# Second block's recurrence: preparations and scans at a higher scheduler's priority

## The chip, the core and the metric

The kernel runs on one core of a Trainium2 chip. Its engines are TensorE (PE in the profile, with its weight loads as PEld), VectorE (DVE), ScalarE (ACT), GpSimd (POOL) and SyncE (SP, which issues most DMAs). The metric is the device time of one execution in microseconds; an execution that was profiled has its own time beside the span of its trace.

## The reference, cut to what matters

The model is a first block (two layers of mixers with feed-forwards, not touched here) and a second block. The second block projects 512 tokens of width 1024 by w_in (RWKV columns and columns of a short convolution), runs a bidirectional recurrence of 8 heads of 64 over them, projects out and goes through 16 experts. The change concerns the recurrence:

```python
px = modulate_2(rmsnorm(x, norm1_g[l]), sh1, sc1) @ w_in[l]
xr, xk, xv, xw, xa, xgl = split_rwkv(px_rw, shift_mu[l], grid_shift(px_rw, rows))
# rwkv_bidir, for each direction d (forward, reversed), from the context's states:
decay = jnp.exp(-jnp.exp(heads(wl)))
a = heads(jax.nn.sigmoid(a0[d] + xa @ a_up[d]))
kd = k * (1 + (a - 1) * k_a_h)
def step(s, inp):
    r_t, w_t, k_t, v_t, a_t, b_t = inp
    sa = jnp.einsum('bhvk,bhk->bhv', s, a_t)
    s = s * w_t[:, :, None, :] + sa[..., :, None] * b_t[:, :, None, :] + v_t[..., :, None] * k_t[:, :, None, :]
    return s, jnp.einsum('bhvk,bhk->bhv', s, r_t)
# then group norm, bonus, gate, and
x = x + g1 * (jnp.concatenate([a_x, b_x], axis=-1) @ w_out[l])
x = x + g2 * expert_choice_ffn(hx, router_w[l], ...)
```

## The kernel before

The kernel computes the recurrence in chunks of 64 tokens, for two groups of four heads, both directions side by side on the partitions. For a group, `rwkv_prep` makes the operands of all eight chunks, and `rwkv_scan` runs over the chunks one after another.

`rwkv_prep` goes from the shifted k, r, v to transposes of v (L1819), sums of squares (L1840), two small projections (L1863, L1869), and then, for each head, a chain on VectorE and ScalarE that begins at L1866 and has a prefix scan (L1876). PE makes the bonus (L1903) and the products of chunk by chunk (L1930, L1981, L1991, flips L1786, L2005). Last comes the inverse of a unit triangular matrix for each chunk and head: VectorE transposes its blocks (L2045), works through 62 small operations and transposes again (L2062, L2081, L2082); ScalarE copies four blocks of 32x1024; PE multiplies 32x32 blocks (L2089, L2099). I call this last part the inverse.

`rwkv_scan` does for each chunk on PE L2128, then an addition on VectorE, L2139, a copy on ScalarE, L2148, and an addition that makes the next state, which the next chunk's L2128 needs. Beside this chain stand the chunk's outputs y (PE L2160 and L2161, two additions on VectorE).

The w_in projection is a matmul of f32 by f32 in three terms of a high and a low part: a block of 128 output columns is 24 matmuls of 128x512 (L434, L436, L439). VectorE makes the low part of a weight (`wsplit`, 128x1024), and the shift of a result takes VectorE operations of 128x512 (`shift_blk`). When the first preparation begins, w_in blocks for the second group (k1, r1, v1), for the gate and for the short convolution are left; they are the generators `second` and `convs`.

`weave` runs generators alternately, at rates, so that their instructions are emitted in a braid: preparation 0 with `second`; scan 0 with `convs` and the first eight steps of preparation 1; preparation 1 with `tail`; scan 1 with the rest of `tail`. `tail` is the out projection of the convolution part (`out_f32`, L2302), the normalisation and gate of heads 0 to 3 (`heads_out`, L2245, L1178, L1191, L2259), the out projection of those, and the same for heads 4 to 7 (L2324 onwards) with the routing (`route_setup`, L2365). Between scan 0 and preparation 1 the activations `a` are freed, and `A.move` opens new pools in their place.

What is emitted isn't yet the order of an engine. The framework's scheduler sorts each engine's instructions, by what is ready by its own estimates and by a priority, which is the place in the emitted order unless something raises it. Each engine then executes in the order it was given, one after another. Arithmetic and allocation in these generators are not touched.

Of the kernel before, what the change touches and what calls it, by code (L numbers as in the profile page):

```python
# [16 lines left out]
TL, TC, TA = 512, 256, 768  # L17
# [149 lines left out]
def _run(g):  # L167

    try:
        while True:  # L170
            next(g)
    except StopIteration as e:
        return e.value
# [186 lines left out]
class _K:  # L360
# [1906 lines left out]
    def braid(self, *gs, first=False):  # L2267
# [17 lines left out]
            yield  # L2285
        return out

    def weave(self, *gs, first=False):

        out = _run(self.braid(*gs, first=first))  # L2290
        self.in_zone(0)
        return out
# [138 lines left out]
    def block2(self):  # L2431
# [15 lines left out]
        heads = lambda g: list(range(4 * g, 4 * g + 4))  # L2447
# [10 lines left out]
        def second(k, r, v, bx):  # L2458
            yield from gemms(1, k, r, v)
            xg = self.shift_blk(aa, 13, TL)  # L2460
            self.act(xg.a, xg.a, AF.Tanh, scale=0.5)
            nc.vector.tensor_scalar(xg.a, xg.a, 1.0, None, op0=OP.add)
            yield
            yield from convs(bx, 0, 2)
            return xg

        def convs(bx, n0, n1):
            for n in range(n0, n1):
                bx.append((yield from self.conv2(aa, n)))

        def some(g, n):
            for _ in range(n):
                next(g)
                yield

        B.zone = [0] * 3 + [1] * (8 - 3)
        wa = self.shift_blk(aa, 12, TL, bank=banks.pop(0))
        self.act(wa.a[0:64], wa.a[0:64], AF.Tanh)
        y, bon = [A.new([4, TL], top=True)], [[A.new([TL], top=True) for _ in range(2)]]
        k, r, v = [], [], []  # L2480
# [1 line left out]
        A.reserve(1, 22528)  # L2482
        none = [None, None]
        k1, r1, v1, bon1, bx = list(none), list(none), list(none), list(none), []
        ops0, xg = self.weave((1, 1, self.rwkv_prep(TL, heads(0), r, k, v, wa, bon[0], lambda: y[0].a), 71),
                              (0, 0, second(k1, r1, v1, bx), 15))
        self.free(v)
        A.unreserve(1)
        A.reserve(2, 2048)
        prep = self.rwkv_prep(TL, heads(1), r1, k1, v1, wa, bon1, lambda: y[1].a)  # L2490
        self.weave((2, 1, self.rwkv_scan(TL, 4, ops0, self.S.a[:, 0:4], y[0].a), 12), (0, 0, convs(bx, 2, 4), 5),
                   (0, 0, some(prep, 8), 8))
        self.free(a)
        A.move(53184, 49984, 52672)
# [13 lines left out]
        def tail():  # L2508
            if 0 == 0:
                yield from self.out_f32(I["w2out"], [(4, b)], x, self.P2, 2, True)  # L2510
            o = yield from self.heads_out(0, y[0], bon[0], xg, center, gup)
            yield from self.out_f32(I["w2out"], [(0, o)] if 0 == 0 else [(4, b), (0, o)], x, self.P2, 2, False)
            self.route_setup()

            w = self.load(I["w2out"][:, :, 2:4, :].rearrange("n q k m -> q n k m"), True)
            for cs, nc in ((slice(1, 3), 6), (slice(0, 4, 3), 8)):
                while self.chunks < nc:
                    yield
                o = yield from self.heads_part(1, y[1], bon[1], xg, center, gup, cs)
                yield from self.out_part(w, o, x, self.P2, 2, cs)  # L2520
                yield from self.route(x, cs)
            w.free()
            self.softmax()

        tail = tail()
        ops1 = self.weave((0, 0, prep, 53), (0, 1, tail, 12), first=True)[0]
        self.free([v1[2:], wa])
        self.weave((2, 0, self.rwkv_scan(TL, 4, ops1, self.S.a[:, 4:8], y[1].a), 18), (0, 1, tail, 14))
        self.free([self.S, self.wlora, self.trim, self.rst64])
        A.unreserve(2)  # L2530
        B.zone = [0] * 8
# [253 lines left out]
```

## Time and profile before

| | us |
|---|---|
| median of 3 runs | 3016.4 |
| lowest and highest | 3009.22, 3019.16 |
| profiled execution | 3014.73 |
| its span in the trace | 3013.0 |
| preparation 0 and its inverse | 2065 to 2228 |
| scan 0 | 2228 to 2274 |
| last w_in matmul ends | 2291 |
| preparation 1 and its inverse | 2291 to 2424 |
| scan 1 | 2424 to 2460 |
| rest of the block, routing | 2460 to 2520 |
| experts, to the end | 2520 to 3013 |

The profiled execution's time is 1.7 us above its span and 1.7 us below the median. The stages are read from the trace by the lines named above; they overlap in the program, so each limit is that of the instruction that the stage's chain begins or ends with.

### The profile page before, as it was taken

To read this page: it belongs to the slowest core of one execution; us is meant where nothing else is said; L and a number is where in the kernel's file an instruction comes from. 1 tells how busy PE (TensorE), PEld (TensorE's weight loads), DVE (VectorE), ACT (ScalarE), POOL (GpSimd) and SP (SyncE) were. 2 spreads that over 40 slices of the span, in tenths; PEclk is the share of its full clock that TensorE was granted. 3 is DMA by queue.
4 is the path that set the end of the run, shared out by engine and by line. 5 is a ranking of instruction groups with operands and counts; after the bars stand their busy time and mean duration, and the time that the engine had idled before them with its cause. 6 is when DMAs were issued, how large, how long until landed. Compare 5 with 4: busy or idle time off the path is not lost.

```text
span 3013.0 us, 43714 instructions
## 1 busy us (share of the span) xinstructions
PE 2833.2 (94%) x17880; PEld 2055.9 (68%) x17880; DVE 1667.0 (55%) x2692; ACT 1025.6 (34%) x1657; POOL 257.9 (9%) x237
## 2 busy tenths in 40 slices
PE   7989999999999999999999999979898898999997
PEld 4877557887888878666588777867675664344443
DVE  5856547776576354677664784367846643221113
ACT  5522335511211135544553522256443522001011
POOL 1034320000000010121000000010010111000000
PEclk9999999999999999999999999989999898999998
DMA  6334452366466103111322222203213045999998
GB/s 221 105 105 115 134 187 86 119 208 207 148 223 214 43 31 109 35 37 42 119 71 84 77 91 70 85 31 128 75 47 111 33 155 207 409 409 409 409 409 293
DMA packets 170441, 458.99 MB, mean 152 GB/s; under 512 B 20176, under 2 KB 52560, under 8 KB 169856
## 3 DMA queue, kind: packets, MB, share of 16 engines
q1 hardware_dynamic: 170240, 456.19, 43.1%
q8 instruction: 140, 2.29, 0.3%
q14 instruction: 61, 0.50, 0.1%
HBM read 441.35 MB, written 14.78 MB: 151 GB/s over the span
## 4 chain that ended last, share of the span: by engine, by line
PE 67%; DVE 12%; DMA 5%; ACT 4%; issue 3%; POOL 0%; SPq 0%; DVEq 0%; ACTq 0%; POOLq 0%
PE ps L434 13%; PE ps L436 12%; PE ps L439 12%; PE ps L2642 9%; DVE mem L389 7%; ACT mem L381 4%; PE ps L2625 2%; DVE mem L392 2%; DMA mem<-in_wadt_dram 1%; PE ps L1624 1%; PE ps L610 1%; PE ps L1119 1%; PE ps L1786 1%; PE ps L2302 1%; DMA mem<-in_eu_dram 1%
## 5 line engine op out<-in xcount | busy, mean ns | idle before, releaser
L381 ACT ACTIVATE mem<-mem 128x1024 fp32r<-128x1024 f32 (+16 forms) x837 | 577.4, 720 | 875.5 <-PE ps L439 215.8
L389 DVE TENSOR_TENSOR mem<-mem,mem 128x1024 fp32r<-128x1024 f32 (+17 forms) x596 | 504.0, 862 | 363.9 <-ACT mem L381 166.6
L381 ACT ACTIVATE mem<-ps 128x512 f32<-128x512 f32 (+8 forms) x591 | 302.0, 527 | 930.8 <-PE ps L439 323.3
L434 PE MATMUL ps<-mem,mem 128*128 128x512 f32 (+3 forms) x1991 | 599.0, 358 | 18.0 <-ACT mem L381 13.9
L436 PE MATMUL ps<-mem,mem 128*128 128x512 f32 (+2 forms) x1906 | 569.5, 354 | 1.0 <-DVE mem L389 0.9
L439 PE MATMUL ps<-mem,mem 128*128 128x512 f32 (+2 forms) x1977 | 417.1, 352 | 0.0
L434 PEld LDWEIGHTS ps<-mem,mem 128*128 128x128 f32 (+2 forms) x1991 | 340.0, 189 | 85.8 <-ACT mem L381 20.6
L436 PEld LDWEIGHTS ps<-mem,mem 128*128 128x128 f32 (+1 forms) x1906 | 327.0, 189 | 60.3 <-issue 6.7
L439 PEld LDWEIGHTS ps<-mem,mem 128*128 128x128 f32 (+1 forms) x1977 | 323.8, 189 | 56.1 <-issue 4.1
L2642 PE MATMUL ps<-mem,mem 128*64 128x512 f32 x1344 | 307.1, 596 | 1.1 <-ACT mem L381 0.8
L436 PE MATMUL ps<-mem 128*128 128x512 f32 (+1 forms) x814 | 271.0, 363 | 0.9 <-POOL mem L389 0.6
L434 PE MATMUL ps<-mem 128*128 128x512 f32 (+1 forms) x729 | 252.8, 371 | 15.0 <-ACT mem L381 11.0
L389 POOL TENSOR_TENSOR mem<-mem 128x256 f32<-128x256 f32 (+4 forms) x72 | 96.0, 1335 | 1828.8 <-ACT mem L381 1417.3
L389 DVE TENSOR_TENSOR mem<-mem,ps 128x512 f32<-128x512 f32 (+5 forms) x234 | 128.9, 581 | 200.7 <-PE ps L2642 103.4
L389 DVE TENSOR_TENSOR mem<-mem 128x512 f32<-128x512 f32 (+21 forms) x370 | 194.8, 533 | 75.0 <-ACT mem L381 23.0
L2642 PEld LDWEIGHTS ps<-mem,mem 128*64 128x64 f32 x1344 | 106.6, 136 | 176.8 <-issue 164.8
L389 DVE TENSOR_TENSOR mem<-ps,mem 128x512 f32<-128x512 f32 (+6 forms) x212 | 133.9, 647 | 103.8 <-PE ps L1111 34.7
L439 PE MATMUL ps<-mem 128*128 128x512 f32 (+3 forms) x743 | 172.1, 361 | 0.0
L436 PEld LDWEIGHTS ps<-mem 128*128 128x128 f32 x814 | 151.6, 193 | 27.3 <-issue 2.5
L434 PEld LDWEIGHTS ps<-mem 128*128 128x128 f32 x729 | 138.0, 194 | 46.4 <-ACT mem L381 16.4
L389 POOL TENSOR_TENSOR mem<-mem,mem 128x512 f32<-128x512 f32 (+6 forms) x88 | 116.6, 1333 | 527.3 <-ACT mem L381 411.0
L392 DVE SCALAR_TENSOR_TENSOR mem<-ps,mem 128x256 f32<-128x256 f32 (+1 forms) x232 | 114.6, 532 | 75.9 <-PE ps L439 75.6
(301 smaller groups left out, 2837.8 us busy)
## 6 DMA issues: line engine op xcount, KB each, us to landing
mem<-in_eg_dram SPq DMA_DIRECT2D x128, 512.0 KB, 10.2
mem<-in_eu_dram SPq DMA_DIRECT2D x128, 512.0 KB, 10.2
mem<-in_ed_dram SPq DMA_DIRECT2D x128, 512.0 KB, 10.2
mem<-in_wadt_dram SPq DMA_DIRECT2D x96, 512.0 KB, 4.3
mem<-in_wup_dram SPq DMA_DIRECT2D x44, 512.0 KB, 3.5
mem<-in_wgate_dram SPq DMA_DIRECT2D x44, 512.0 KB, 3.5
mem<-in_wdown_dram SPq DMA_DIRECT2D x40, 512.0 KB, 3.5
mem<-in_w2in_dram SPq DMA_DIRECT2D x35, 512.0 KB, 4.0
```

The costliest lines, as they stand in the source:

```text
L381: return self.nc.scalar.activation(out, in_, func, **kw)
L389: return (eng or self.nc.vector).tensor_tensor(out, a, b, op=op)
L392: return self.nc.vector.scalar_tensor_tensor(out, a, s, b, op0=op0, op1=op1)
L434: mm(o, w(0, k), acts[k][0][:, ts], start=(k == 0), stop=False)
L436: mm(o, w(0, k), acts[k][1][:, ts], start=False, stop=False)
L439: mm(o, w(1, k), acts[k][0][:, ts], start=False, stop=(k == nk - 1))
L610: nc.tensor.matmul(b.a[32 * q:32 * q + 32, :], cs.a[:, k, :], raw.a[:, j * 512:(j + 1) * 512], start=(k == 0), stop=(k == 7))
L1119: mm(out[half[i]], vv, w.a[:, i, :], start=(J == 0), stop=(J == last))
L1624: m = mm(po.a[64 * i:64 * i + 64, :], v.a[:, kb, 64 * h:64 * h + 64], pt.a[:, i, :], start=(kb == 0), stop=(kb == 5))
L1786: self.nc.tensor.matmul(out, src, i, start=True, stop=True)
L2625: mm(b.a[:, :256], ht.a[:, c, fs], o, start=(c == 0), stop=(c == 3))
L2642: mm(bk.a[64 * i:64 * i + 64, 512 * n:512 * n + 512], lhs(k, i), w[i][:, 512 * n:512 * n + 512], start=(k == 0), stop=(k == 7))
```

## The change

A new helper `urgent` runs each step of a generator at a priority 4000 places ahead of its own. It is put around the two preparations and the two scans. Instructions, tiles and buffers are the same; what differs is the order on each engine from some 2065 us on.

```diff
@@ -2285,6 +2285,16 @@
             yield
         return out
 
+    def urgent(self, g):
+
+        while True:
+            with self.tc.high_priority(4000):
+                try:
+                    next(g)
+                except StopIteration as e:
+                    return e.value
+            yield
+
     def weave(self, *gs, first=False):
 
         out = _run(self.braid(*gs, first=first))
@@ -2482,13 +2492,13 @@
         A.reserve(1, 22528)
         none = [None, None]
         k1, r1, v1, bon1, bx = list(none), list(none), list(none), list(none), []
-        ops0, xg = self.weave((1, 1, self.rwkv_prep(TL, heads(0), r, k, v, wa, bon[0], lambda: y[0].a), 71),
+        ops0, xg = self.weave((1, 1, self.urgent(self.rwkv_prep(TL, heads(0), r, k, v, wa, bon[0], lambda: y[0].a)), 71),
                               (0, 0, second(k1, r1, v1, bx), 15))
         self.free(v)
         A.unreserve(1)
         A.reserve(2, 2048)
-        prep = self.rwkv_prep(TL, heads(1), r1, k1, v1, wa, bon1, lambda: y[1].a)
-        self.weave((2, 1, self.rwkv_scan(TL, 4, ops0, self.S.a[:, 0:4], y[0].a), 12), (0, 0, convs(bx, 2, 4), 5),
+        prep = self.urgent(self.rwkv_prep(TL, heads(1), r1, k1, v1, wa, bon1, lambda: y[1].a))
+        self.weave((2, 1, self.urgent(self.rwkv_scan(TL, 4, ops0, self.S.a[:, 0:4], y[0].a)), 12), (0, 0, convs(bx, 2, 4), 5),
                    (0, 0, some(prep, 8), 8))
         self.free(a)
         A.move(53184, 49984, 52672)
@@ -2525,7 +2535,7 @@
         tail = tail()
         ops1 = self.weave((0, 0, prep, 53), (0, 1, tail, 12), first=True)[0]
         self.free([v1[2:], wa])
-        self.weave((2, 0, self.rwkv_scan(TL, 4, ops1, self.S.a[:, 4:8], y[1].a), 18), (0, 1, tail, 14))
+        self.weave((2, 0, self.urgent(self.rwkv_scan(TL, 4, ops1, self.S.a[:, 4:8], y[1].a)), 18), (0, 1, tail, 14))
         self.free([self.S, self.wlora, self.trim, self.rst64])
         A.unreserve(2)
         B.zone = [0] * 8
```

The rows of the engines' order below give line, operation, output and inputs, shape and how many in a row; `mem_76` are the split weights, `mem_13623` and `mem_15860` pools of this block, `mem_64` a pool of long-lived tiles, `ps` the accumulators. Lines behind the new helper are ten higher after the change (L2312 is L2302, L2375 is L2365, L2334 is L2324).

The first place is PE where the inverse of heads 0 to 3 begins (L2089). Before the change:

```order
L434 MATMUL ps<-mem_76 128x512
L436 MATMUL ps<-mem_76 128x512
L439 MATMUL ps<-mem_76 128x512 x8
L2005 MATMUL ps<-mem_64,mem_13623 64x64 x24
L434 MATMUL ps<-mem_76 128x512
L1786 MATMUL ps<-mem_64,mem_13623 64x64 x10
L2089 MATMUL ps<-mem_13623,mem_64 32x32 x16
L1786 MATMUL ps<-mem_64,mem_13623 64x64 x6
L436 MATMUL ps<-mem_76 128x512
L434 MATMUL ps<-mem_76 128x512
L2089 MATMUL ps<-mem_13623,mem_64 32x32 x16
```

After it:

```order
L436 MATMUL ps<-mem_76 128x512
L434 MATMUL ps<-mem_76 128x512
L436 MATMUL ps<-mem_76 128x512
L434 MATMUL ps<-mem_76 128x512
L436 MATMUL ps<-mem_76 128x512
L434 MATMUL ps<-mem_76 128x512
L2089 MATMUL ps<-mem_13623,mem_64 32x32 x64
L436 MATMUL ps<-mem_76 128x512
L434 MATMUL ps<-mem_76 128x512
L436 MATMUL ps<-mem_76 128x512
L2099 MATMUL ps<-mem_13623 32x32 x32
```

Before, one w_in block ends, the last products (L2005) follow, and then the inverse's matmuls come with w_in matmuls (L434, L436) between every few. After, L2005 and the flips stand farther ahead, 68 w_in matmuls come in one piece, and the inverse's matmuls come 64 and 32 in a row.

The second place is DVE, in a chunk of scan 0. The addition with output 128x256 from `ps,mem_13623` is the one that L2139 waits for; that from `ps,mem_64` makes the next state; 64x4x64 are the y additions. Before:

```order
L389 TENSOR_TENSOR mem_64<-ps,mem_13623 128x256
L389 TENSOR_TENSOR mem_64<-ps,mem_64 128x256
L389 TENSOR_TENSOR mem_64<-mem_64,ps 64x4x64 x2
L389 TENSOR_TENSOR mem_64<-ps,mem_13623 128x256
L389 TENSOR_TENSOR mem_64<-ps,mem_64 128x256
L389 TENSOR_TENSOR mem_64<-mem_64,ps 64x4x64 x2
```

After:

```order
L389 TENSOR_TENSOR mem_64<-ps,mem_13623 128x256
L389 TENSOR_TENSOR mem_64<-mem_64,ps 64x4x64 x2
L389 TENSOR_TENSOR mem_64<-ps,mem_64 128x256
L389 TENSOR_TENSOR mem_64<-ps,mem_13623 128x256
L389 TENSOR_TENSOR mem_64<-mem_64,ps 64x4x64 x2
L389 TENSOR_TENSOR mem_64<-ps,mem_64 128x256
```

Before, the two y additions of a chunk stand ahead of the next chunk's first addition; after, they stand behind it.

The third place is PE at the end of scan 1. Before:

```order
L2128 MATMUL ps<-mem_64,mem_13623 64x64 x8
L2160 MATMUL ps<-mem_13623,mem_64 64x64
L2302 MATMUL ps<-mem_15860 128x512
L2139 MATMUL ps<-mem_64,mem_13623 64x64 x8
L2302 MATMUL ps<-mem_15860 128x512
L2161 MATMUL ps<-mem_13623,mem_64 64x64
L2160 MATMUL ps<-mem_13623,mem_64 64x64
...
L2160 MATMUL ps<-mem_13623,mem_64 64x64
L2161 MATMUL ps<-mem_13623,mem_64 64x64
L2365 MATMUL ps<-mem_64 128x32 x8
L2324 MATMUL ps<-mem_64 64x256 x4
```

After (from the fifth chunk on, and its end):

```order
L2128 MATMUL ps<-mem_64,mem_13623 64x64 x8
L2160 MATMUL ps<-mem_13623,mem_64 64x64
L2312 MATMUL ps<-mem_15860,mem_15864 128x512
L2139 MATMUL ps<-mem_64,mem_13623 64x64 x8
L2312 MATMUL ps<-mem_15860,mem_15864 128x512
...
L2160 MATMUL ps<-mem_13623,mem_64 64x64
L2161 MATMUL ps<-mem_13623,mem_64 64x64
L2312 MATMUL ps<-mem_15860 128x512 x6
L2375 MATMUL ps<-mem_64 128x32 x8
L2334 MATMUL ps<-mem_64 64x256 x4
```

Before, out-projection matmuls stand in the gaps of every chunk, and L2365 follows the last y product. After, six of them are left over behind the last y product and stand ahead of L2365.

## Rows read from the trace of the kernel before

**Rows 1.** page, its first line: the whole span

```profile
span 3013.0 us, 43714 instructions
```

**Rows 2.** windows by stage: from:to, length, busy (records) by engine, clock, DMA share, GB/s

```profile
core 0: us, PE busy (x) PEld busy (x) DVE busy (x) ACT busy (x) POOL busy (x), PEclk, DMA share, GB/s
2065.40:2141.40 76.00, 68.93 (x459) 48.69 (x458) 62.51 (x96) 45.14 (x77) 5.37 (x4) 0.98 0.21 71
2141.40:2192.80 51.40, 47.06 (x598) 38.11 (x599) 45.04 (x97) 26.21 (x43) 0.00 (x0) 0.93 0.23 77
2192.80:2227.60 34.80, 33.07 (x505) 27.39 (x503) 14.31 (x16) 19.92 (x23) 2.21 (x2) 0.85 0.18 55
2227.60:2274.30 46.70, 46.70 (x711) 36.69 (x710) 17.49 (x35) 12.81 (x23) 8.11 (x12) 1.00 0.12 37
2274.30:2291.40 17.10, 17.10 (x96) 14.50 (x96) 6.60 (x14) 4.94 (x7) 0.00 (x0) 1.00 0.08 31
2291.40:2378.20 86.80, 73.27 (x734) 42.71 (x735) 74.50 (x135) 42.90 (x79) 14.40 (x12) 0.92 0.33 103
2378.20:2388.10 9.90, 5.05 (x89) 3.04 (x87) 6.70 (x6) 8.61 (x6) 0.75 (x2) 0.94 0.29 101
2388.10:2410.00 21.90, 21.90 (x236) 16.60 (x237) 6.42 (x17) 7.55 (x13) 1.24 (x1) 0.50 0.01 1
2410.00:2423.70 13.70, 13.70 (x252) 11.81 (x254) 3.20 (x5) 4.14 (x7) 0.00 (x0) 0.72 0.45 152
2423.70:2460.10 36.40, 36.40 (x638) 23.94 (x637) 17.74 (x36) 3.07 (x8) 8.04 (x12) 1.00 0.36 117
2460.10:2520.50 60.40, 45.15 (x216) 32.27 (x216) 37.16 (x103) 24.54 (x54) 14.26 (x14) 0.74 0.52 184
2520.50:3009.00 488.50, 464.63 (x2132) 214.89 (x2132) 90.91 (x164) 51.08 (x96) 1.27 (x1) 0.99 0.97 379
```

**Rows 3.** timeline of PE: ends of two w_in blocks, and the last block

```profile
2055.03 1.98 PE L439 MATMUL ps<-mem 128*128 128x512 f32 x8
2060.47 0.84 PE L439 MATMUL ps<-mem 128*128 128x512 f32 x3
...
2289.36 1.98 PE L439 MATMUL ps<-mem 128*128 128x512 f32 x8
```

**Rows 4.** timeline of ACT and DVE behind the last w_in matmul (start, length)

```profile
2291.44 1.15 ACT L381 ACTIVATE mem<-mem 128x512 f32<-128x512 f32 x2 [5.00 <-PE ps L439]
...
2294.62 0.43 DVE L1866 TENSOR_SCALAR mem<-mem 128x512 f32<-128x512 f32 x1 [0.32 <-ACT mem L381]
...
2296.22 0.67 DVE L392 SCALAR_TENSOR_TENSOR mem<-mem,mem 128x512 f32<-128x512 f32 x1
```

**Rows 5.** timeline of PE in the first preparation, waits in brackets

```profile
2126.93 1.47 PE L1903 MATMUL ps<-mem,mem 128*64 128x512 f32 x2 [3.27 <-DVE mem L392]
...
2143.83 1.33 PE L1930 MATMUL ps<-mem 64*64 64x128 f32 x16 [2.54 <-ACT mem L381]
```

**Rows 6.** timeline of the second inverse: ACT's copies and PE's wait

```profile
2379.42 7.87 ACT L381 ACTIVATE mem<-mem 32x1024 f32<-32x1024 f32 x4 [2.83 <-DVE mem L2062]
...
2388.05 1.97 PE L2245 MATMUL ps<-mem 128*64 128x512 f32 x2 [4.84 <-ACT mem L381]
```

**Rows 7.** timeline of one chunk of scan 0, PE and DVE

```profile
2265.16 0.63 PE L2128 MATMUL ps<-mem,mem 64*64 64x64 f32 x15
2265.36 0.85 DVE L389 TENSOR_TENSOR mem<-mem,ps 64x256 f32<-64x256 f32 x2 [0.33 <-PE ps L2161]
2266.25 0.42 DVE L389 TENSOR_TENSOR mem<-ps,mem 128x256 f32<-128x256 f32 x1
...
2269.89 0.63 PE L2128 MATMUL ps<-mem,mem 64*64 64x64 f32 x15
```

**Rows 8.** timeline of PE: an out-projection pair in scan 1, and L2324

```profile
2436.91 1.12 PE L2302 MATMUL ps<-mem 128*128 128x512 f32 x2
...
2461.92 1.08 PE L2324 MATMUL ps<-mem 128*64 128x256 f32 x8
```

## The prediction

> **What bounds the kernel now.** I read the windows by stage first, because the change begins at about 2065 us of a span of 3013.0 us [rows 1] and a share over the whole span says nothing of this part. The reader should see three regimes in [rows 2]. From 2065.4 to 2291.4 TensorE is busy for 212.9 of 226.0 us (the first five rows added up): it is the bound, and what it does between the recurrence's small products is the w_in matmuls of 128x512. From 2291.4 to 2460.1 those are used up and the recurrence of heads 4 to 7 is a chain: VectorE is busy for 74.50 of 86.80 us, TensorE idles, and then TensorE runs at a granted clock of 0.50 and 0.72. From 2520.5 to the end the DMA share is 0.97 with 379 GB/s: the experts' weights stream, so whatever moves the end of the second stretch moves the end of the kernel by as much.
>
> Next I looked for what holds the two stretches apart. ScalarE's first operation of the second head group that writes into the pools moved behind the w_in work is released by the last w_in matmul, after 5.00 us of idle, and VectorE's first step of the chain follows at 2294.62 [rows 4]. Both orders have this pool there. So the second chain starts 3.3 us after the last w_in matmul (which ends at 2289.36 + 1.98 = 2291.34, [rows 3]) in either order, and the case falls into two sums: how late the last w_in matmul is, and how long the chain behind it takes.
>
> **Sum A, up to the last w_in matmul.** The work of TensorE ahead of that matmul is the same set of instructions; the change only puts the recurrence in front and the w_in matmuls behind. Nothing is removed, so this time changes only by idle time and clock. A block of 24 w_in matmuls takes 2060.47 − 2055.03 = 5.44 us [rows 3], 0.227 us each. I counted them in both orders (661 behind the same starting point): at the start of the triangular inverse of heads 0 to 3 it is 470 before and 430 after; at the first product of scan 0 it is 517 and 435; at the end of scan 0 it is 607 and 475. So 132 matmuls, 29.9 us, come out from among the recurrence and stand in one piece behind scan 0. Whether that is free depends on what is left as cover, stage by stage:
>
> - Preparation of heads 0 to 3, 2065.4 to 2192.8: idle now is 7.1 + 4.3 us. Forty matmuls (9.1 us) leave. What gets shorter for it is VectorE's queue, busy for 62.51 of 76.00 us: of 12 shift operations (one of that kind and size takes 0.67 us at 2296.22 in [rows 4]) that stood ahead of the first transposes, 5 stay, 4.7 us less. In the second half VectorE has no fewer of other work in front (15 shift operations and 6 splits against 8 and 7, and a few of the convolution). So the matmuls leave 9.1 us, the chain gives at most 4.7: extra idle between −4 (some waits such as the 3.27 us on VectorE and 2.54 us on ScalarE of [rows 5] go) and +9. I take +3, nearer to 9.1 − 4.7.
> - The inverse, 2192.8 to 2227.6: 47 matmuls (10.7 us) of its 34.8 us shrink to 5 (1.1 us), while 68 w_in matmuls (15.4 us) now stand in one piece ahead of it. ScalarE's four copies ahead of its products take 7.9 us (the same copies of the second group, [rows 6]), shorter than these 15.4 us, so they are covered: idle 0 to +4, I take +0.5.
> - Scan 0, 2227.6 to 2274.3: full now. 90 matmuls become 40, so 50 x 0.227 = 11.4 us leave and 35.3 us of TensorE work stay. The chain of one chunk is 2269.89 − 2265.16 = 4.73 us [rows 7], 37.8 us for eight. It gets shorter, since the addition that the chain waits for now stands ahead of the two y additions (0.85 us) on VectorE, and TensorE takes the next chunk's first product ahead of most y products. Eight times 0.3 to 1.0 us makes 30 to 35 us: about the work that is left, idle 0 to +3, I take +0.5.
> - Behind scan 0, 186 matmuls (42.2 us) follow, with five splits and the last shifts on VectorE: idle 0 to +4, I take +0.5.
> - Clock: now 0.93, 0.85 and 1.00 in the three stages. Where it falls to 0.50, as at 2388.1, the 22.4 us of small products of the inverse (33.07 − 10.7) could take up to 9 us more. I take 0; it goes into the range.
>
> Sum A: +4.5, from −4 to about +13 with the ends not all at once.
>
> **Sum B, from there to the route.** The section from 2291.4 to the last y product is 168.7 us.
>
> - VectorE's chain, 2291.4 to 2378.2, comes in another order (the four heads step by step instead of one after another), with the same operations; it was busy for 74.50 of 86.80 us. What can go is idle time such as that ahead of the first transposes: 0 to −5, I take −1.
> - The inverse, 2378.2 to 2423.7: TensorE idles 4.84 us behind ScalarE's four copies [rows 6], and then works 21.90 us at clock 0.50. In the new order the normalisation of heads 0 to 3 (L2245, L1178, L1191, L2259), which stood here, is in scan 1; eight out-projection matmuls are spread up to here. At half clock L2245 takes 1.97 us twice, and the others some 4 us. So −8; 0 if the idle time grows by what leaves, −15 if the clock comes back too (the 21.90 us at full clock would be some 11).
> - Scan 1, 36.4 us: the normalisation comes in, at full clock about 4 us in gaps that are there; chunks may be shorter by what scan 0's are. Out-projection matmuls inside fall from 16 to 10, and six now stand behind the last y product and ahead of L2365. One is 1.12 us (two records, [rows 8]), 6.7 us in all, and the work that the end waits for, L2324, follows behind. Scan −2 (−5 to +8, the upper end if the first four chunks, without 128-wide matmuls now, run at half clock), tail +6.7.
>
> Sum B: −1 − 8 − 2 + 6.7 = −4.3, from −16 to +10.
>
> **The sum.** +4.5 − 4.3 = 0. The profiled execution took 3014.73 us, 1.7 below the median of 3016.4; I forecast 3017 for the median. A measurement tells some 9 us (0.3%) from no change.
>
> The trace shows what the clock does: 4.84 us without work, then 21.90 us of unbroken work at 0.50, which is the 1.2 GHz level, and 1.00 again by scan 1 [rows 2, 6]. The Trainium skill ("TensorE: Matmul & The Clock Gate", section "Why this matters for your kernels") says beside this that gaps between bursts of matmuls drop the clock to its lower level, and that dense matmul work brings it back. By that rule the change speaks against itself in the first head group, where it takes the dense matmuls out from among the small ones; the time it gives is that of the second rival. The trace so far agrees with it only at 2388.1; scan 0's small products at 1.00 had w_in matmuls among them.
>
> **Rivals.**
>
> 1. *Faster.* The out-projection matmuls and the moved normalisation close the gap at 2383 and the clock stays up in the second inverse. Then its 45.5 us lose the 4.84 us of idle, and the 21.90 + 13.70 us at 0.50 and 0.72 shrink by some 11 + 4; less the tail of 6.7 us and Sum A at +1 that is about −13: 3003. For it: the new order does put the work there. Against: ScalarE's copies still run 7.9 us between VectorE's transposes and the first product, and what is put ahead of them may be done before they begin.
> 2. *Slower.* TensorE's queue is in order, and w_in matmuls no longer stand between the recurrence's products, so TensorE waits for VectorE and ScalarE in the first preparation (+9), the inverse and scan (+4), and the lower clock follows into the small products (+5), and in Sum B the tail of 6.7 us takes back what the moved normalisation gives. Decisive is whether idle time from 2065 to the last w_in matmul grows beyond the 13.1 us of now by more than 9. That is some +18: 3034. For it: TensorE was the bound in this stretch, and a bound engine gains nothing from another order. Against: a few w_in matmuls still stand in nearly every gap of the new order (40 of them in scan 0), and now VectorE serves the chain first.
>
> **Chances.** The forecast (3007 to 3025, the 30 us taken out and given back) 0.44, rival 1 0.26, rival 2 0.30. The range reaches to the far sides of both rivals, −17 to +21: 3000 to 3038. Faster by over 0.3% 0.26, within 0.44, slower 0.30.
>
> **What would show it.** The last w_in matmul (L439) at 2291 to 2301, with VectorE's L1866 of the second group 3 us behind it. Scan 0's end at some 2245 to 2252 instead of 2274, from which about 42 us of unbroken w_in matmuls follow. The step from the second group's last transposes to scan 1 at 35 to 40 us instead of 45.5, and six L2302 in a row ahead of L2365. The experts' stretch as long as now. I am wrong if the second chain starts well ahead of the last w_in matmul (then Sum A is worth up to 30 us of gain), if the experts' weights come in earlier and the last stretch gets shorter, or if the clock is at 0.5 through scan 0 and scan 1.

## The result, and the profile after

The changed kernel takes 3049.64 us (median; 3048.29 to 3054.11, 4 runs) against 3014.23 us before (3009.22 to 3019.16, 4 runs): a ratio of 1.0115, 95% interval 1.0100 to 1.0129. It is slower by some 35 us, outside the forecast's range and beyond the second rival. The profiled execution has a span of 3048.4 us, 35.4 more than before [rows 1].

Windows by stage after the change; the limits are the same instructions as in [rows 2] (the 5.00 us from 2489.3 are a stage of their own now):

```profile
core 0: us, PE busy (x) PEld busy (x) DVE busy (x) ACT busy (x) POOL busy (x), PEclk, DMA share, GB/s
2065.40:2144.40 79.00, 69.27 (x451) 49.07 (x449) 59.28 (x91) 44.30 (x76) 4.98 (x4) 0.94 0.18 57
2144.40:2194.70 50.30, 44.84 (x719) 38.89 (x720) 45.58 (x101) 26.30 (x46) 0.00 (x0) 0.93 0.33 107
2194.70:2221.00 26.30, 23.91 (x328) 20.03 (x327) 10.83 (x10) 16.00 (x17) 1.33 (x2) 0.60 0.15 40
2221.00:2254.20 33.20, 32.63 (x609) 25.36 (x608) 14.71 (x31) 4.30 (x9) 8.05 (x12) 0.96 0.08 28
2254.20:2311.46 57.26, 57.26 (x281) 44.78 (x279) 16.79 (x25) 18.58 (x27) 0.00 (x0) 0.94 0.13 42
2311.50:2410.00 98.50, 75.13 (x835) 45.96 (x836) 74.41 (x138) 40.73 (x78) 15.09 (x12) 0.90 0.29 92
2410.00:2449.70 39.70, 38.48 (x434) 26.43 (x435) 8.62 (x11) 16.76 (x19) 2.53 (x2) 0.66 0.16 51
2449.70:2489.30 39.60, 38.98 (x665) 26.73 (x660) 21.18 (x47) 7.17 (x15) 8.47 (x12) 1.00 0.42 146
2489.30:2494.30 5.00, 5.00 (x12) 2.14 (x12) 2.27 (x4) 0.00 (x0) 0.00 (x0) 1.00 0.89 299
2494.30:2554.80 60.50, 46.10 (x220) 32.80 (x219) 38.12 (x104) 24.51 (x54) 14.22 (x14) 0.72 0.43 151
2554.80:3044.00 489.20, 465.87 (x2131) 215.89 (x2129) 89.95 (x161) 51.04 (x96) 1.27 (x1) 0.98 0.96 378
```

Read against [rows 2], the last row is as long as before (489.2 and 488.5 us), so the loss lies ahead of the experts. Two rows stand out: 57.26 us of TensorE work behind scan 0 (42.2 were forecast, for the w_in matmuls alone; the sums of squares of heads 4 to 7, 4.83 us, and a few other products stand in it too), and 98.50 us for the second preparation instead of 86.80. The inverse behind it is shorter (39.70 us, before 9.90 + 21.90 + 13.70 = 45.5), scan 1 longer.

Profiled executions differ by some microseconds ahead of the stretch that the change touches, so the two sums are read from a landmark just ahead of it, TensorE's last L481 (2018.65 us before, 2022.30 after). From there to the end of the last w_in matmul, before:

```profile
2018.65:2291.34 272.69, 255.50 (x2585) 202.20 (x2584) 180.50 (x311) 133.69 (x211) 15.69 (x18) 0.96 0.24 80
```

and after:

```profile
2022.30:2311.46 289.16, 266.96 (x2588) 211.48 (x2587) 179.91 (x311) 132.82 (x211) 14.37 (x18) 0.91 0.23 76
```

That is 16.5 us more: TensorE is busy for 11.5 us more with the same work (2585 and 2588 records), at a mean clock of 0.91 instead of 0.96, and idles for 22.2 instead of 17.2 us. As an estimate, length times the missing share of the clock is 0.09 x 289.16 = 26 us after and 0.04 x 272.69 = 11 us before; this counts idle time at the lower clock too, so it is rough. From the last w_in matmul to L2365 (L2375 after) it is 182.8 us (2311.5 to 2494.3) instead of 168.7: 14.1 more. The remaining 5 us of the 35.4 lie ahead of the landmark (3.6) and behind the routing.

TensorE's timeline shows what the lower clock does, in the first inverse and behind L1840, the sums of squares of heads 4 to 7:

```profile
2207.08 3.43 PE L2099 MATMUL ps<-mem 32*32 32x32 f32 x64
2212.37 1.12 PE L2128 MATMUL ps<-mem,mem 64*64 64x64 f32 x16
2221.03 1.12 PE L2139 MATMUL ps<-mem,mem 64*64 64x64 f32 x16
...
2286.29 4.83 PE L1840 MATMUL ps<-mem,mem 128*128 128x2 f32 x32
2294.54 2.43 PE L439 MATMUL ps<-mem 128*128 128x512 f32 x8
```

L2139 takes 1.12 us for the 16 records that take 0.68 us later in the same scan, and eight w_in matmuls behind L1840 2.43 us instead of the 1.98 of [rows 3].

VectorE's timeline in the second preparation; before, where [rows 4] has the first L1866 at 2294.62:

```profile
2319.09 0.42 DVE L1866 TENSOR_SCALAR mem<-mem 128x512 f32<-128x512 f32 x1
2320.08 1.22 DVE L1876 TENSOR_TENSOR_SCAN mem<-mem,mem 128x512 f32<-128x512 f32 x1
...
2340.74 1.24 DVE L2045 STREAM_TRANSPOSE mem<-mem 64x1024 f32<-64x1024 f32 x1 [3.22 <-ACT mem L381]
```

and after:

```profile
2314.75 0.43 DVE L1866 TENSOR_SCALAR mem<-mem 128x512 f32<-128x512 f32 x1 [0.52 <-ACT mem L381]
2318.65 0.40 DVE L1866 TENSOR_SCALAR mem<-mem 128x512 f32<-128x512 f32 x1
2321.52 0.41 DVE L1866 TENSOR_SCALAR mem<-mem 128x512 f32<-128x512 f32 x1
...
2336.35 1.22 DVE L1876 TENSOR_TENSOR_SCAN mem<-mem,mem 128x512 f32<-128x512 f32 x1
...
2341.81 0.69 DVE L389 TENSOR_TENSOR mem<-mem,ps 128x512 f32<-128x512 f32 x1 [1.85 <-PE ps L1903]
2345.00 0.69 DVE L392 SCALAR_TENSOR_TENSOR mem<-mem,mem 128x512 f32<-128x512 f32 x1 [2.50 <-ACT mem L381]
2349.26 0.69 DVE L389 TENSOR_TENSOR mem<-mem 64x512 f32<-64x512 f32 x1 [2.72 <-POOL mem L389]
...
2371.89 1.24 DVE L2045 STREAM_TRANSPOSE mem<-mem 64x1024 f32<-64x1024 f32 x1 [2.49 <-ACT mem L381]
```

The chain starts 3.3 us behind the last w_in matmul, as before. But four heads now begin within 7 us (L1866 at 2314.75 to 2321.52; before 2294.62 to 2319.09, one head after another). The fourth head's prefix scan (2336.35) comes 15 us behind its L1866 (before 1 us), since the operations of three heads stand between, and later VectorE waits for TensorE, ScalarE and GpSimd. The first transposes (L2045) come 57.1 us behind the chain's start; before it was 46.1. The windows of these two stretches, columns as above, before and after:

```profile
2294.62:2340.74 46.12, 35.77 (x227) 17.41 (x225) 40.91 (x60) 22.01 (x42) 9.21 (x8) 0.89 0.48 151
2314.75:2371.89 57.14, 39.84 (x278) 20.69 (x276) 39.96 (x60) 22.23 (x43) 11.76 (x9) 0.85 0.39 129
```

VectorE does the same 60 operations in 40.91 and 39.96 us. What grew is its idle time, from 5.2 to 17.2 us.

TensorE's timeline there:

```profile
2316.74 1.12 PE L1863 MATMUL ps<-mem 64*128 64x512 f32 x2
2332.34 2.07 PE L2312 MATMUL ps<-mem,mem 128*128 128x512 f32 x2 [14.48 <-DMA mem<-in_w2out_dram]
2334.62 1.95 PE L1903 MATMUL ps<-mem,mem 128*64 128x512 f32 x2 [0.21 <-DVE mem L392]
...
2342.07 1.12 PE L2312 MATMUL ps<-mem,mem 128*128 128x512 f32 x2
2343.12 1.12 PE L1869 MATMUL ps<-mem 64*128 64x512 f32 x2
```

and SyncE's queue:

```profile
2311.50 4.59 SPq L1805 DMA_DIRECT2D mem<-scratch  x6
...
2327.25 1.09 SPq L1805 DMA_DIRECT2D mem<-scratch  x2
2328.39 0.58 SPq L404 DMA_DIRECT2D mem<-scratch  x1
2329.01 0.43 SPq L404 DMA_DIRECT2D mem<-in_w2out_dram  x1
```

TensorE waits 14.48 us for a w_out tile. Its load stands on SyncE behind the last two copies of r (L1805), which wait for VectorE until 2327.25, and behind TensorE's waiting L2312 stands, among others, the fourth head's L1869.

The end of scan 1 on TensorE:

```profile
2489.05 5.42 PE L2312 MATMUL ps<-mem 128*128 128x512 f32 x12
2494.31 1.87 PE L2375 MATMUL ps<-mem 128*128 128x32 f32 x16
2496.11 1.08 PE L2334 MATMUL ps<-mem 128*64 128x256 f32 x8
```

The six left-over out-projection matmuls (twelve records) hold L2375 up for 5.26 us.

### The profile page after: what moved, and what is told of

Its sections match the earlier page's. It is cut to its first block, busy times and chain, and to the rows that moved or that the text cites. A ratio compares the mean times of both kernels' runs of the same rounds, so it can differ in the third digit from the quotient of the medians.

```text
span 3048.4 us, 43743 instructions
## 1 busy us (share of the span) xinstructions
PE 2856.8 (94%) x17880; PEld 2068.0 (68%) x17880; DVE 1667.6 (55%) x2692; ACT 1022.8 (34%) x1657; POOL 258.4 (8%) x237
## 4 chain that ended last, share of the span: by engine, by line
PE 66%; DVE 10%; issue 6%; DMA 5%; ACT 4%; POOL 0%; SPq 0%; DVEq 0%; ACTq 0%; POOLq 0%
PE ps L434 12%; PE ps L436 12%; PE ps L439 12%; PE ps L2652 9%; DVE mem L389 5%; ACT mem L381 3%; PE ps L2635 2%; DMA mem<-in_wadt_dram 1%; PE ps L1624 1%; DVE mem L392 1%; PE ps L1786 1%; PE ps L1930 1%; PE ps L610 1%; DMA mem<-in_ed_dram 1%; PE ps L2312 1%
## 5 line engine op out<-in xcount | busy, mean ns | idle before, releaser
L434 PE MATMUL ps<-mem,mem 128*128 128x512 f32 (+3 forms) x1991 | 598.1, 357 | 16.5 <-ACT mem L381 12.3
L436 PE MATMUL ps<-mem,mem 128*128 128x512 f32 (+2 forms) x1906 | 567.9, 353 | 0.9 <-DVE mem L389 0.9
L434 PEld LDWEIGHTS ps<-mem,mem 128*128 128x128 f32 (+2 forms) x1991 | 338.5, 189 | 84.6 <-ACT mem L381 19.5
L436 PEld LDWEIGHTS ps<-mem,mem 128*128 128x128 f32 (+1 forms) x1906 | 326.2, 189 | 60.2 <-issue 6.7
L436 PE MATMUL ps<-mem 128*128 128x512 f32 (+1 forms) x814 | 271.6, 363 | 1.4 <-POOL mem L389 1.0
L434 PE MATMUL ps<-mem 128*128 128x512 f32 (+1 forms) x729 | 253.9, 372 | 13.7 <-ACT mem L381 10.5
L436 PEld LDWEIGHTS ps<-mem 128*128 128x128 f32 x814 | 152.0, 194 | 29.3 <-issue 3.6
L434 PEld LDWEIGHTS ps<-mem 128*128 128x128 f32 x729 | 138.3, 194 | 46.3 <-ACT mem L381 15.8
```

Source lines behind the costliest of these rows:

```text
L434: mm(o, w(0, k), acts[k][0][:, ts], start=(k == 0), stop=False)
L436: mm(o, w(0, k), acts[k][1][:, ts], start=False, stop=False)
```

## Experiments

Columns of the table: median and ratio to the runs of before on the same chip (95% interval); from one profiled execution of each, and so without a spread, the time from the last L481 to the last w_in matmul (A), from the second chain's first L1866 to the first L2045 (chain), and from that to the routing (rest). "Kept" means that the steps of a generator keep their own order, "mixed" that they don't, as told below. In e12_prep1_lost0 and e15_all_lost0 the routing's L2365 stands ahead of the end of scan 1, so there "rest" isn't comparable; behind L2365 these two are 9 and 43 us longer than before, the others at most 4.

| run | what is ahead | us | ratio | A | chain | rest |
|---|---|---|---|---|---|---|
| before | nothing | 3014 to 3018 | 1 | 272.7 | 46.1 | 119.3 |
| the change | all four, mixed | 3049.64 | 1.0115 (1.0100 to 1.0129) | 289.2 | 57.1 | 122.4 |
| e1_prep0 | preparation 0, mixed | 3027.07 | 1.0031 (1.0019 to 1.0044) | 283.9 | 47.3 | 122.4 |
| e2_scan0 | scan 0 | 3021.3 | 1.0007 (0.9994 to 1.0021) | 276.2 | 48.3 | 118.3 |
| e3_prep1 | preparation 1, mixed | 3040.07 | 1.0070 (1.0053 to 1.0086) | 278.1 | 57.2 | 123.9 |
| e4_scan1 | scan 1 | 3017.88 | 1.0000 (0.9986 to 1.0013) | 273.1 | 46.1 | 119.3 |
| e5_early | e3, w_out loads early | 3042.38 | 1.0098 (1.0066 to 1.0130) | 281.3 | 55.3 | 128.0 |
| e6_skip8 | e3 without its first 8 steps | 3039.75 | 1.0077 (1.0054 to 1.0101) | 274.3 | 57.8 | 123.1 |
| e7_inv | e1, its inverse put back | 3047.0 | 1.0109 (1.0085 to 1.0134) | 295.7 | 46.7 | 121.4 |
| e9_skip8_early | e5 and e6 | 3037.23 | 1.0072 (1.0048 to 1.0095) | 274.6 | 54.9 | 128.8 |
| e10_all_kept | all four, kept | 3034.54 | 1.0058 (1.0038 to 1.0078) | 282.4 | 49.7 | 117.5 |
| e11_prep1_kept | preparation 1, kept | 3028.11 | 1.0042 (1.0025 to 1.0059) | 278.7 | 49.9 | 120.4 |
| e12_prep1_lost0 | nothing; preparation 1 mixed | 3046.42 | 1.0097 (1.0077 to 1.0117) | 277.4 | 59.8 | 119.2 |
| e13_prep0_kept | preparation 0, kept | 3025.5 | 1.0034 (1.0019 to 1.0049) | 274.8 | 48.0 | 119.4 |
| e14_prep0_lost0 | nothing; preparation 0 mixed | 3075.32 | 1.0195 (1.0170 to 1.0220) | 323.8 | 46.3 | 120.8 |
| e15_all_lost0 | nothing; all four mixed | 3137.07 | 1.0403 (1.0381 to 1.0425) | 365.1 | 59.2 | 91.2 |
| e16_skip8_kept | e11 without its first 8 steps | 3025.56 | 1.0034 (1.0021 to 1.0046) | 274.4 | 50.0 | 120.5 |

**One part at a time.** The change with `urgent` left around one generator:

```diff
 # e1_prep0: the other three without urgent; e2_scan0, e3_prep1, e4_scan1 likewise
-prep = self.urgent(self.rwkv_prep(TL, heads(1), ...))
+prep = self.rwkv_prep(TL, heads(1), ...)
```

e1_prep0: 

> Priority on preparation 0 alone. Theory (small products without w_in matmuls among them idle and run at the lower clock, in preparation 0 and its inverse): last w_in matmul 10 to 15 us later than before, whole time +10 to +15. Rival (scan 0 bare of w_in matmuls is what costs): within 4 us of before.

e2_scan0: 

> Priority on scan 0 alone. Theory: scan 0 ends earlier, its w_in matmuls follow, 0 to +4 us. Rival (scan 0 bare of w_in matmuls is what costs in the first stretch): +10 or more.

e3_prep1: 

> Priority on preparation 1 alone. Theory (copies of k and r queued ahead of the w_out loads on SyncE hold these up, TensorE waits for the first w_out tile with the chain's L1869 behind it): last w_in matmul as before or up to 4 us later, first transposes 10 us later than before, whole time +8 to +14. Rival (order on VectorE, head by head against step by step, is what costs): also later, but without a wait of TensorE for a w_out load.

e4_scan1: 

> Priority on scan 1 alone. Theory: three out-projection matmuls instead of two behind the scan, so within 2 us of before. Rival (scan 1 itself is slower in its new order): +5 or more.

The parts add up: 0.31 + 0.07 + 0.70 + 0.00 = 1.08%, against 1.15%. The scans cost nothing that can be told; the preparations cost all of it, the second more than twice the first. Scan 1 alone moves time only: in its run the stretch from L2062 to scan 1 falls from 45.5 to 39.0 us and scan 1 grows from 36.4 to 42.9. The expectations of e2_scan0 and e4_scan1 held, that of e1_prep0 nearly (+11.2 us up to the last w_in matmul, +9.6 in the median). e3_prep1 lost more than was expected, 0.70% or 21 us. Of these 21 us, 5.4 show ahead of the last w_in matmul and 11 in the chain; the late w_out tile is there too (14.18 us of waiting).

**Is it the late load?** In e5_early the loads of `out_f32` get a place farther ahead, in e6_skip8 the steps that run beside scan 0 keep their place, e9_skip8_early has both:

```diff
 # e5_early, in out_f32
-raws, b = [self.load(w[n, :, k0:k0 + len(bs), :]) for k0, bs in parts], self.B.new()
+with self.tc.high_priority(8000):
+    raws = [self.load(w[n, :, k0:k0 + len(bs), :]) for k0, bs in parts]
+b = self.B.new()
 # e6_skip8, in urgent, for preparation 1
-with self.tc.high_priority(4000):
+with self.tc.high_priority(4000) if n > 8 else nullcontext():
```

e5_early: 

> As the run with preparation 1 alone, with the loads of w_out tiles of the out projection issued at a still higher priority, so that they stand ahead of the copies of k and r on SyncE. Theory (the blocked loads cost preparation 1 some 11 us): TensorE's wait of 14 us for a w_out tile shrinks under 4 us, first transposes follow the chain's start by 46 to 50 us instead of 57, whole time 8 to 12 us below that run. Rival (order on VectorE or the eight L2312 in a row): at most 3 us below it.

e6_skip8: 

> As the run with preparation 1 alone, but its first eight steps, which run beside scan 0, keep their own priority. Theory (those steps' sums of squares, put into scan 0, cost the 8 us by which the last w_in matmul was late): last w_in matmul within 2 us of before, whole time 5 to 9 us below the run with preparation 1 alone. Rival (the late w_in matmul is no loss for the end): less than 3 us below.

e9_skip8_early: 

> Both edits of the two runs before it together, on preparation 1 alone. Theory (the two costs are separate): last w_in matmul as before, chain behind it no longer than before, the second inverse some 5 us shorter: between 3014 and 3021, at most 0.1% above before. Rival (the order of the products itself costs): 0.3% or more above before.

All three theories fell (e6_skip8's on the whole time). TensorE in e9_skip8_early (L2316 is the out projection there):

```profile
2304.90 5.31 PE L2316 MATMUL ps<-mem,mem 128*128 128x512 f32 x6 [3.60 <-DMA mem<-scratch]
2319.07 1.97 PE L1903 MATMUL ps<-mem,mem 128*64 128x512 f32 x2 [8.86 <-DVE mem L392]
...
2327.88 1.12 PE L1869 MATMUL ps<-mem 64*128 64x512 f32 x2
```

TensorE's wait in front of the out projection is down from 14.48 us (14.18 in e3_prep1) to 3.60, and ends with a load from scratch, no longer of w_out; but L1903 now waits 8.86 us for VectorE, and the fourth head's L1869 is still 29.7 us behind the chain's start (28.4 in the change). The chain takes 54.9 us, 8.8 more than before. The late load was a symptom that stood beside another wait. e6_skip8 brings the last w_in matmul back (274.3), without a gain in the whole time that can be told from e3_prep1.

**Is it the inverse without w_in matmuls?** e7_inv puts the last transposes and the products of the inverse in preparation 0 4000 places back, so that w_in matmuls stand one by one between them:

```diff
 # e7_inv, around the last transposes and each round of products in tri_inverse
+with self.tc.high_priority(-4000) if self.hot else nullcontext():
```

> As the run with preparation 0 alone, but the inverse's products of heads 0 to 3 are put 4000 places back, so that w_in matmuls stand one by one between them. Theory (the inverse without w_in matmuls runs at the lower clock and loses 5 us or more): clock of the inverse 0.85 or more instead of 0.6, whole time 3 to 7 us below the run with preparation 0 alone. Rival (idle time in the preparation's products is all of it): within 2 us of that run.

It went the other way, 0.78% above the run with preparation 0 alone (1.0109 and 1.0031). Windows of 15 us in its inverse:

```profile
2205.00:2220.00 15.00, 15.00 (x113) 8.16 (x112) 5.79 (x7) 2.37 (x4) 0.31 (x1) 1.00 0.13 36
2220.00:2235.00 15.00, 15.00 (x76) 7.22 (x76) 0.00 (x0) 1.82 (x3) 1.02 (x2) 0.52 0.05 19
2235.00:2250.00 15.00, 15.00 (x169) 11.82 (x168) 2.25 (x3) 4.12 (x7) 0.00 (x0) 0.50 0.16 56
```

From 2220 TensorE is busy for all 15.00 us at 0.52, though w_in matmuls of 128x512 stand between the 32x32 products (one every 0.97 us); the expectation that they keep the clock up is wrong in this form (the scopes of −4000 give the place counter back too, see below, so its two rounds of products also mix with each other). The clock isn't all of it: in the window ahead, at 1.00, the two kinds already alternate, and a w_in matmul with two 32x32 products takes 0.60 us. In a row, at the same clock, the w_in matmul is 0.227 us and 26 of the small ones are 0.62. So each such alternation costs some 0.33 us more (an estimate from these three figures).

**The order of a generator's own steps.** The fine mixture in the engines' orders led to the scope itself. Printed while the program is built, for five steps of preparation 0 in a row: the place counter at the start of a step, inside the scope at its start and end, and after the scope:

```
13722 9722 9727 13722
13722 9722 9727 13722
13722 9722 9727 13722
13722 9722 9727 13722
13756 9756 9776 13756
```

The scope gives the counter back at its end. Steps of one generator that follow each other, up to the next step of another one, therefore start at the same place (the first four rows), and the scheduler mixes them: that is where the four heads in step come from. Two variants, each around different generators, separate this from being ahead (loop and return cut):

```diff
 # kept (e10_all_kept, e11_prep1_kept, e13_prep0_kept): what a generator has issued so far is taken off
+n, tc = 0, self.tc
-    with self.tc.high_priority(4000):
+    with tc.high_priority(4000 - n):
+        p = tc.cur_priority
         next(g)
+        n += tc.cur_priority - p
 # mixed without being ahead (e12_prep1_lost0, e14_prep0_lost0, e15_all_lost0)
-    with self.tc.high_priority(4000):
+    with self.tc.high_priority(0):
```

e10_all_kept: 

> All four generators ahead as in the change, but each step is put 4000 places ahead less what its generator has issued so far, so that the steps keep their own order. Theory (the scope gives back the place counter at its end, so that steps of a generator start at the same place and their instructions mix; that mix is what costs, the 4000 places are not): 0 to +10 us against before instead of +35. Rival (to be ahead of w_in and out-projection work is what costs): +25 or more.

e11_prep1_kept: 

> Preparation 1 alone, ahead with its steps in their own order. Theory: chain's start to first transposes 44 to 49 us as before, not 57, whole time within 5 us of before. Rival (being ahead costs): +15 us or more, as the run with preparation 1 alone.

e12_prep1_lost0: 

> Preparation 1 alone, with the scope around each step at an offset of 0 places: not ahead, but the steps start at the same place and mix. Theory: the loss of the run with preparation 1 alone shows without any place gained, +10 us or more, first transposes 54 us or more behind the chain's start. Rival: as before within 4 us.

e13_prep0_kept: 

> Preparation 0 alone, ahead with its steps in their own order. Theory (mix of steps costs): within 4 us of before. Rival (w_in matmuls missing in the inverse, at the lower clock, cost the 9 us): +6 to +12, with the stretch from the last transposes to scan 0 some 9 us longer than before.

e14_prep0_lost0: 

> Preparation 0 alone with the scope at an offset of 0: steps mix, nothing is put ahead. Theory (in preparation 0 the missing w_in matmuls cost, not the mix): within 4 us of before, last w_in matmul less than 3 us later. Rival (the mix costs here as in preparation 1): +8 or more.

e15_all_lost0: 

> All four generators with the scope at an offset of 0 places: steps mix, nothing is put ahead. Theory (two costs, the mix of steps in preparation 1 and w_in matmuls taken from preparation 0 and scan 0): the mix alone gives +20 to +32 us. Rival (the mix costs only where the 4000 places come with it): under +12.

e16_skip8_kept: 

> Preparation 1 alone, ahead, its steps in their own order, and the first eight steps (beside scan 0) left at their own place. Theory (what was left of the loss with the order kept, some 12 us, is half the sums of squares in scan 0): last w_in matmul as late as before, whole time +3 to +8 us against before. Rival (the loss left is all behind the last w_in matmul): +10 or more.

VectorE in e11_prep1_kept, where the heads come one after another again:

```profile
2307.98 0.43 DVE L1866 TENSOR_SCALAR mem<-mem 128x512 f32<-128x512 f32 x1 [0.52 <-ACT mem L381]
2313.04 0.42 DVE L1866 TENSOR_SCALAR mem<-mem 128x512 f32<-128x512 f32 x1
2321.04 0.42 DVE L1866 TENSOR_SCALAR mem<-mem 128x512 f32<-128x512 f32 x1
2333.33 0.42 DVE L1866 TENSOR_SCALAR mem<-mem 128x512 f32<-128x512 f32 x1
2357.89 1.24 DVE L2045 STREAM_TRANSPOSE mem<-mem 64x1024 f32<-64x1024 f32 x1 [3.22 <-ACT mem L381]
```

From the first L1866 to L2045 it is 49.9 us instead of 57.2 (e3_prep1). With the order kept, the whole change costs 0.58% instead of 1.15%, preparation 1 alone 0.42% instead of 0.70%. With the order lost and nothing put ahead, preparation 1 costs 0.97%, preparation 0 1.95% and the four together 4.03%; the last two are far outside what was expected (within 4 us, and 20 to 32 us). So the lost order is costly by itself, and the 4000 places hide a part of that cost.

The mix costs in two ways, and the runs tell them apart. In preparation 1 it is the chain on VectorE. In preparation 0 it is TensorE: at an offset of 0 a step also shares its places with the w_in steps emitted beside it, and its products come out alternating with w_in matmuls. The inverse in e14_prep0_lost0, and its window from the landmark L481 to the last w_in matmul:

```profile
2223.55 0.24 PE L2089 MATMUL ps<-mem,mem 32*32 32x32 f32 x2
2223.72 0.51 PE L434 MATMUL ps<-mem 128*128 128x512 f32 x1
2224.15 0.24 PE L2089 MATMUL ps<-mem,mem 32*32 32x32 f32 x2
```

```profile
2026.85:2350.63 323.78, 309.24 (x2585) 226.80 (x2584) 179.79 (x311) 133.30 (x211) 14.76 (x18) 0.89 0.20 68
```

TensorE idles less than before (14.5 and 17.2 us) and is busy for 53.7 us more with the same 2585 records. Between a w_in matmul and another product it changes 268 times in that window, before 108 times (e15_all_lost0: 398, the change: 97). As an estimate, 160 changes more are 80 alternations of 0.33 us, 26 us, and the clock (0.89 and 0.96) takes some 25 us more; together 51, and 51.1 is what the window grew by. For e15_all_lost0 the same sum (clock 0.85) gives 92 us, where 92.4 were measured, for e7_inv (172 changes, clock 0.90) 29, where it was 23.0. Put ahead, the preparation leaves most w_in matmuls behind it and this alternation doesn't arise.

But being ahead costs too: the expectations for the runs with kept order (at most 10 us for all four, 5 for preparation 1, 4 for preparation 0) were passed, at ratios of 1.0058, 1.0042 and 1.0034. In preparation 0 the run with kept order and the one with mixed order can't be told apart when they are ahead (0.34 and 0.31%). e16_skip8_kept leaves 1.0034, so the sums of squares in scan 0 are not all that is left of preparation 1's loss.

## Why the prediction was wrong, point by point

**What held.** The regimes: the experts' stretch is as long as before, and every microsecond passed through. The second chain starts 3.3 us behind the last w_in matmul. Idle time up to there was put at +4.5 us and measured at +5.0, and by stage too ([rows 2] against the windows after: preparation +3.8, inverse +0.7, scan +0.6, behind it 0; forecast +3 and three times +0.5). Scan 0 ends at 2254 (forecast some 2245 to 2252; the changed trace is 3.6 us late already at the landmark), the inverse takes 39.7 us (35 to 40), and the tail behind scan 1 is 5.26 us (6.7). The first sign failed: the last w_in matmul ends at 2311.5, not 2291 to 2301.

**The step that failed** is the first of Sum B: the chain of preparation 1 comes "in another order (the four heads step by step instead of one after another), with the same operations", and so can only lose idle time, 0 to −5 us. It measured +11.0: VectorE's operations took no longer than before, and its idle time grew by 12.0 us instead of shrinking. The order lay open before the run, but only its operations were counted. Their places matter, since VectorE's queue is worked off in order: with three heads in step, the first head's products are ready late (the first L1903 19.9 us behind the chain's start, in e11_prep1_kept 9.1), and the fourth head's prefix scan waits behind three heads' work. That the mixed order costs this is shown: 59.8 us with the mixed order alone (e12_prep1_lost0), 57.2 and 49.9 with the same generator ahead, mixed and kept (e3_prep1, e11_prep1_kept). The 3.8 us by which 49.9 is above 46.1 come with being ahead, not with the mix. The cause that the trace seemed to name, the late w_out load, was not it, or only for 2 to 3 us: with the load early the chain still takes 55.3 and 54.9 us, against 57.2 and 57.8 without (e5_early and e9_skip8_early, e3_prep1 and e6_skip8). That the places are lost through the scope's counter was overlooked altogether: the change was taken to put a generator ahead as a whole.

**A mis-sized term, of equal weight.** In Sum A the clock was put at 0, with up to 9 us left for the range. TensorE's busy time to the last w_in matmul grew by 11.5 us with the same work, at a mean clock of 0.91 instead of 0.96. Together with the idle time this is +16.5, where +4.5 was forecast and +13 was the end of the range. The second rival came near that number for another reason: its 18 us were 13 of idle time and 5 of clock, measured were 5.0 and 11.5. By its own test (idle time up by more than 9 us) it fell, so its nearness in Sum A is luck. Nor did it have the chain: it expected nothing from Sum B, which measured +14.1.

On the rule cited from the Trainium skill ("TensorE: Matmul & The Clock Gate", section "Why this matters for your kernels"), that gaps between bursts of matmuls lower the clock: the trace of the change agrees in the first inverse, which begins with 2.39 us of idle and runs at 0.60. e7_inv doesn't fit it: there the clock falls from 1.00 to 0.52 and 0.50 with TensorE busy for 15.00 of 15.00 us in all three windows.

**Also off.** Scan 1 was put at −2 and took 39.6 us, 3.2 more. The moved normalisation was put at −8 in the inverse and gave −5.8. e4_scan1 shows what such a move is worth: nothing, 6.4 us less and 6.5 more.

**Open.** Why being ahead costs 0.3 to 0.6% with the order kept: in e10_all_kept it is +9.7 us up to the last w_in matmul (5.6 busy, 4.1 idle, at a mean clock of 0.93 instead of 0.96) and +3.6 in the chain (where TensorE's clock is 0.76, before 0.89), but no run separates clock from idle time. What lowers the clock in stretches in which TensorE is busy throughout was not settled.

## What to carry to other kernels

A priority scope that gives its counter back doesn't only put work ahead, it also makes the pieces inside equal among themselves; where a generator is wrapped step by step, look in the new order whether its own steps still follow each other, and carry what was issued over into the next scope. On an engine with an in-order queue, chains worked in step finish all of them late, which here left VectorE waiting for the engine that needed the first result. Small products alternating with large matmuls one by one cost TensorE time even where its clock stays up. Where the engine was already the bound (here TensorE, busy for 94% of that stretch), putting the chain ahead of the filler gained nothing, even with the order kept.

## What was not expected of the hardware

Thirty-two matmuls of two columns each (L1840) took 4.83 us after the change and 3.63 us before, and the w_in matmuls behind them ran at the lower level for some time: the window from 2285 to 2295 had a granted clock of 0.68 with TensorE busy for 10.00 of 10.00 us, while the 5.70 us that held the same 32 before had 1.00. In e7_inv 32x32 products alternating with w_in matmuls ran some 15 us at 1.00 and then, with no idle time between, at 0.52 and 0.50. At 1.00 such a pair of kinds took 0.60 us where the same matmuls in a row take some 0.27. A busy TensorE in the profile is no sign of the clock that it is granted.
